# The first projection stage in another order: gates last, the 1/rms row ahead of them, evictions of q, k and v that wait one by one

## The chip, the cores and the metric

The kernel runs on one core of a Trainium2 chip. The metric is the device time of one execution in microseconds. Engines are named as in the profile: PE is TensorE, DVE is VectorE, ACT is ScalarE, POOL is GpSimd, SP is SyncE, whose queue issues most DMAs.

## What is computed

One encoder block on x of 1024 positions by 1024 channels, float32. The part around the change is the beginning:

```python
h = rms_norm(x, norm_mix)
proj = h @ w_in                                  # 1024 x 3104
q, k, v, z, b_f, b_b, a_f, a_b, su, sv = split(proj, [512]*4 + [8]*4 + [512]*2)
qkv = silu(short_conv([q, k, v], conv_w))        # 5 taps along the positions
o_a = bidir_gated_deltanet(qkv, z, b_f, b_b, a_f, a_b, ...)   # 8 heads x 64, chunks of 64
o_b = spatial_gating(su, sv, ...)                # 4 groups x 128, chunks of 128
x = x + [o_a, o_b] @ w_out
x = x + square(relu(rms_norm(x, norm_ffn) @ w_ff1)) @ w_ff2
return rms_norm(x, norm_final)
```

The four small columns b and a (32 in all) are the gates. In the DeltaNet each chunk needs a decay matrix from the gates, Gram products of q and k, and a triangular solve.

## The kernel before

Every large product is done as three float32r matmuls (`mm3`: high x high, high x low, low x high), since each operand is split into a rounded high part and a rest. The rms norm is not applied to x: the products run on x times the gain, and the results are scaled by 1/rms when they leave PSUM. For q, k and v, which come with channels on the partitions, that takes a row of 1/rms for 1024 positions on all partitions, `rrow`.

**First stage** (`first`, L214). Eight steps over the contraction (`dt`). Each loads a piece of x transposed (512 KB, split into `xh` and `xl`) and a piece of weights `w0` (416 columns: 128 each of q, k, v of head pair 0, and the 32 gate columns). x is squared on ACT and summed on DVE into `sqs`. The eight PSUM banks are all taken: `qkv[0..5]` (q, k, v, two halves of the positions each) and `gate[0..1]`. In each step PE does the gates' six matmuls and then 18 for q, k, v. Behind the last step: eight matmuls with a column of ones sum the squares over the partitions (L259), POOL takes the power -0.5 (L262), DVE multiplies the identity with it (`dg`, L265), and two matmuls of a full matrix of ones with `dg` make the row (L272), both into the bank `gate[0]`, copied out by L273. The gates are transposed (L269) and scaled (L275).

**Projections** (`project`, L301). The other columns in the order z, pair 1 (q, k, v), pair 2, a, pair 3, b, where a and b are the two halves of the gating unit's columns. A z, a or b item has eight blocks of 24 matmuls, a q, k or v item two. A block uses one bank of a ring of three (`psd`), and its eviction is put into program order when the block behind it is issued (`flush(1)`). q, k and v are evicted by DVE times `rrow` (`evac_qkv`, L379) into a buffer `cx` of which there are two, z and a, b by ACT. Before a q, k or v item the program waits until the convolution two items back has read its buffer (`self.taps`). Weights come through `piece` (L152): SP loads a raw tile (two buffers), ACT writes the high part and the negated copy, and a POOL DMA adds the source onto it (L164); there are nine buffers `w`. With `early=True` POOL subtracts instead (L149).

**Side lanes.** `conv` (four taps of DVE, L472, behind ACT's first, L469), `heads` (transposes, L495), `gates`, `prep` (decay matrices: matmul L561, exponential L562), `stage1` (Gram products L594, then the solve: L611, L619, 30 steps of L625 and L627, transposes L635 and L637, merge L645 and L657) are generators that say what they cost. `run` lays them beside the projections by those costs, and the scheduler of the framework then orders each engine's queue by priorities and by what is ready in its own model of time. The solves of the four pairs follow one another. `outproj` starts when all of them are done. Then comes the MLP.

The lines that wait and evict before:

```python
yield lambda: n < 0 or n in self.taps      # at the start of a q, k, v item; n = p * 3 + j - 2
...
late.append((self.evac_qkv, ps, x, h, p, j))
flush(1)
```

Of the kernel before, what the change touches and what calls it, by code (L numbers as in the profile page):

```python
# [10 lines left out]
F32 = mybir.dt.float32  # L11
# [3 lines left out]
ALU = mybir.AluOpType  # L15
# [4 lines left out]
P = 128  # L20
# [33 lines left out]
class Kern:  # L54
# [159 lines left out]
    def first(self, xp):  # L214

        nc, a, tkx, tkp = self.nc, self.a, self.tkx, self.tkp
        N = 3 * P + 32
        tmp = tkp.tile([P, 1024], F32, tag="V", name="tmp")
# [23 lines left out]
        self.w0 = [self.piece(a["wt"][0, dt]) for dt in range(NT)]  # L242
        gT = tmp[0:32]
        for dt in range(NT):
            for h in range(2):
                th = slice(h * 512, h * 512 + 512)
                self.mm3(gate[h][0:32], w[dt][:, 0, 3 * P:N], w[dt][:, 1, 3 * P:N], self.xh[dt][:, th], self.xl[dt][:, th],
                         dt == 0, dt == NT - 1)
                if dt == NT - 1:
                    nc.vector.tensor_copy(gT[:, th], gate[h][0:32])  # L250
            for i in range(6):
                j, h = divmod(i, 2)
                ws, th = slice(j * P, j * P + P), slice(h * 512, h * 512 + 512)
                self.mm3(qkv[i], w[dt][:, 0, ws], w[dt][:, 1, ws], self.xh[dt][:, th], self.xl[dt][:, th],
                         dt == 0, dt == NT - 1)
                if dt == NT - 1 and i == 1:

                    for b in range(NB):
                        nc.tensor.matmul(gate[0][:, b:b + 1], sqs[:, b * P:(b + 1) * P], ones[:, 0:1], start=True, stop=True)  # L259
                    with self.tc.high_priority(offset=400):  # L260
                        nc.vector.tensor_scalar(ss, gate[0][:, 0:NB], 1.0 / D, EPS, ALU.mult, ALU.add)
                        nc.gpsimd.tensor_tensor(self.rstd, ss, self.mhalf.broadcast_to([P, NB]), ALU.pow)  # L262

                        dg = self.sgup.tile([P, NB, P], F32, tag="uv", name="dg", bufs=3)
                        nc.vector.tensor_tensor(dg, self.ident.unsqueeze(1).broadcast_to([P, NB, P]),  # L265
                                                self.rstd.unsqueeze(2).broadcast_to([P, NB, P]), ALU.mult)
                if dt == NT - 1 and i == 2:
                    for b in range(NB):
                        nc.tensor.transpose(gate[1][:, b * 32:b * 32 + 32], gT[:, b * P:b * P + P], self.ident[0:32, 0:32])  # L269
# [18 lines left out]
    def new_cx(self):  # L288
# [3 lines left out]
        return x  # L292

    def third(self):

        yield "dve 1.4"
        x = self.new_cx()
        for h in range(2):
            self.evac_qkv(self.qkv0[4 + h], x, h, 0, 2)

    def project(self):  # L301

        nc = self.nc
        late, self.taps, self.uv = [], set(), 3
# [4 lines left out]
        def loads(kind, p, j):  # L309

            if kind == "q":
                return [self.a["wqkv"][p * 3 + j][:, i * 4:i * 4 + 4] for i in range(2)]
            return [self.a["wt"]["zab".index(kind), dt] for dt in range(NT)]

        def flush(n):
            while len(late) > n:
                f, *args = late.pop(0)
                f(*args)

        for j in range(2):  # L320
            yield "dve 1.4"
            x = self.new_cx()
            for h in range(2):
                self.evac_qkv(self.qkv0[j * 2 + h], x, h, 0, j)
        self.side("conv", self.third())
# [6 lines left out]
        for it, (kind, p, j) in enumerate(items):  # L332
            nxt = []
            after = loads(*items[it + 1]) if it + 1 < len(items) else []
            if kind == "q":
                n = p * 3 + j - 2
                yield lambda: n < 0 or n in self.taps
                todo = after
                for h in range(2):
                    yield "pe 2.6" + (" act 2.4" if todo else "")  # L340
                    load(4 - h)
                    if h == 0:
                        x = self.new_cx()
                    ps = self.psd()
                    th = slice(h * 512, h * 512 + 512)
                    for dt in range(NT):
                        if dt == NT // 2:
                            yield "pe 2.6 dve .6"
                        wd, ws = w[dt // 4], slice(dt % 4 * P, dt % 4 * P + P)
                        self.mm3(ps, wd[:, 0, ws], wd[:, 1, ws], self.xh[dt][:, th], self.xl[dt][:, th],  # L350
                                 dt == 0, dt == NT - 1)
                    late.append((self.evac_qkv, ps, x, h, p, j))
                    flush(1)
            else:
# [3 lines left out]
                for b in range(NB):  # L358
# [17 lines left out]
        flush(0)  # L376

    def evac_qkv(self, ps, x, h, p, j):
        self.nc.vector.tensor_tensor(x[:, 2 + h * 512:514 + h * 512], ps, self.rrow[:, h * 512:h * 512 + 512],  # L379
                                     ALU.mult)  # L380
        if h == 1:
            self.side("conv", self.conv(p, j, x))

# [160 lines left out]
    def prep(self, p):  # L544
# [669 lines left out]
def layouts(i):  # L1214
# [9 lines left out]
    dtile = lambda m, n: c(m.reshape(n, NT // n, P, -1).transpose(0, 2, 1, 3))  # L1224
    r["w0"] = c(np.concatenate([w[:, 0:P], w[:, 512:512 + P], w[:, 1024:1024 + P], w[:, 2048:2080]], 1).reshape(NT, P, -1))
    r["wqkv"] = c(np.stack([dtile(w[:, j * 512 + p * P:j * 512 + (p + 1) * P], 1)[0]
# [34 lines left out]
```

## Time and profile before

| | us |
|---|---|
| median of 3 runs | 1374.23 |
| lowest, highest | 1369.28, 1379.46 |
| the profiled execution | 1376.48 |
| its span, first to last instruction | 1374.7 |
| PE busy | 1312.6 |
| DVE busy | 722.4 |
| ACT busy | 516.7 |
| POOL busy | 245.1 |

The profile is of one execution. A busy time counts an engine's instructions and says nothing of which of them the end waited for; times in the rows are counted from the start of the span. A bracket at the end of a row of the order of time gives the idle time of the engine ahead of the instruction, and what ended it.

### The profile page before, as it was taken

The numbers are of one execution on the slowest core, as the hardware profiler recorded it, in microseconds if no ns is written. First come the engines' busy times: TensorE is split into PE (matmuls) and PEld (weight loads), VectorE is DVE, ScalarE is ACT, GpSimd is POOL, SyncE is SP. The second block draws the span as 40 slices with busy tenths as digits, with TensorE's granted clock in tenths as the row PEclk, the third lists the DMA queues.
The fourth block names the chain that finished last, engine by engine and source line by source line (L and its number), as shares of the span: only waits on it lengthen the run. The fifth ranks groups of instructions, "written<-read, shape, count | busy, mean of one in ns | idle before, by whom it ended". The sixth has DMA issues, their size and how long they took to land.

```text
span 1374.7 us, 20558 instructions
## 1 busy us (share of the span) xinstructions
PE 1312.6 (95%) x8129; PEld 1082.6 (79%) x8129; DVE 722.4 (53%) x1213; ACT 516.7 (38%) x958; POOL 245.1 (18%) x353
## 2 busy tenths in 40 slices
PE   8799899999868899999999999999999999999997
PEld 5588687778767798877788888888888888888885
DVE  6252696969696566777533433434333343343445
ACT  6445755587446554413421311313113131131224
POOL 3301330333385776000000000000000000000013
PEclk9899999999979999999999999999999999999999
DMA  6618753572555653410012101121011210212103
GB/s 230 150 45 256 189 139 73 136 156 70 169 145 113 156 134 90 137 47 1 9 46 69 54 23 54 46 69 54 12 58 54 69 45 10 69 54 69 39 16 130
DMA packets 132464, 119.80 MB, mean 87 GB/s; under 512 B 76144, under 2 KB 96496, under 8 KB 131824
## 3 DMA queue, kind: packets, MB, share of 16 engines
q1 hardware_dynamic: 125168, 105.38, 25.4%
q0 software_dynamic: 6048, 11.01, 5.0%
q10 hardware_dynamic: 1152, 2.10, 0.4%
q8 instruction: 64, 1.05, 0.3%
q14 instruction: 32, 0.26, 0.1%
HBM read 91.71 MB, written 27.33 MB: 87 GB/s over the span
## 4 chain that ended last, share of the span: by engine, by line
PE 79%; DVE 7%; ACT 4%; DMA 4%; issue 2%; POOL 2%; SPq 1%; POOLq 0%; ACTq 0%; DVEq 0%
PE psd L140 14%; PE psd L141 14%; PE psd L142 13%; PE psg L140 9%; PE psg L141 9%; PE psg L142 9%; PE psg L805 3%; PE psg L796 2%; DMA raw<-in_wqkv 1%; DVE lt L625 1%; DVE lane L627 1%; PE pss L850 1%; DVE ca L472 1%; DMA raw<-in_wt 1%; PE psg L594 1%
## 5 line engine op out<-in xcount | busy, mean ns | idle before, releaser
L140 PE MATMUL psg<-fh,w 128*128 128x512 f32 x512 | 199.2, 389 | 0.6 <-DVE fl L1017 0.6
L142 PE MATMUL psd<-w,ff 128*128 128x512 f32 x512 | 199.3, 389 | 0.0
L141 PE MATMUL psd<-w,ff 128*128 128x512 f32 x512 | 199.2, 389 | 0.0
L141 PE MATMUL psg<-fl,w 128*128 128x512 f32 x512 | 199.1, 389 | 0.0
L142 PE MATMUL psg<-fh,w 128*128 128x512 f32 x512 | 198.0, 389 | 0.0
L140 PE MATMUL psd<-w,ff 128*128 128x512 f32 x512 | 195.3, 389 | 0.0
L1091 DVE SCALAR_TENSOR_TENSOR x<-psd,r,x 128x512 f32<-128x512 f32 x128 | 94.5, 749 | 175.7 <-PE psd L142 175.6
L148 ACT CAST w<-raw 128x512 fp32r<-128x512 f32 (+2 forms) x104 | 77.6, 746 | 247.9 <-PE psd L142 125.6
L149 DVE TENSOR_TENSOR w<-raw,w 128x512 fp32r<-128x512 f32 (+1 forms) x96 | 83.5, 870 | 101.2 <-ACT w L148 100.9
L1074 ACT ACTIVATE relu<-psg 128x512 f32<-128x512 f32 x64 | 38.2, 597 | 245.8 <-PE psg L142 245.8
L1049 POOL TENSOR_SCALAR fs<-fs 128x1 f32<-128x1 f32 x8 | 5.6, 694 | 672.0 <-ACT scr L1046 672.0
L140 PEld LDWEIGHTS psg<-fh,w 128*128 128x128 f32 x512 | 96.2, 188 | 20.8 <-DVE fl L1017 0.8
L140 PEld LDWEIGHTS psd<-w,ff 128*128 128x128 f32 x512 | 96.1, 188 | 20.3 <-DVE x L1091 0.4
L141 PEld LDWEIGHTS psd<-w,ff 128*128 128x128 f32 x512 | 96.2, 188 | 20.0
L141 PEld LDWEIGHTS psg<-fl,w 128*128 128x128 f32 x512 | 96.2, 188 | 19.9
L142 PEld LDWEIGHTS psg<-fh,w 128*128 128x128 f32 x512 | 96.1, 188 | 19.9
L142 PEld LDWEIGHTS psd<-w,ff 128*128 128x128 f32 x512 | 96.1, 188 | 20.0
L1075 DVE TENSOR_TENSOR relu<-relu 128x512 f32<-128x512 f32 x64 | 44.2, 691 | 110.3 <-ACT relu L1074 110.3
L140 PE MATMUL psd<-xh,w 128*128 128x512 f32 (+1 forms) x168 | 67.4, 404 | 9.9 <-ACT xh L209 5.5
L140 PE MATMUL psd<-w,xh 128*128 128x512 f32 x192 | 76.6, 400 | 0.0
L141 PE MATMUL psd<-w,xh 128*128 128x512 f32 x192 | 76.2, 397 | 0.0
L142 PE MATMUL psd<-w,xl 128*128 128x512 f32 x192 | 76.1, 396 | 0.0
(238 smaller groups left out, 2424.6 us busy)
## 6 DMA issues: line engine op xcount, KB each, us to landing
raw<-in_w SPq DMA_DIRECT2D x32, 512.0 KB, 3.5
raw<-in_w SPq DMA_DIRECT2D x64, 256.0 KB, 2.7
raw<-in_wt SPq DMA_DIRECT2D x24, 256.0 KB, 3.0
w<-in_wt POOLq DMA_DIRECT2D x24, 256.0 KB, 5.1
tok_d<-tok SPq DMA_DIRECT2D x24, 256.0 KB, 4.8
raw<-in_wqkv SPq DMA_DIRECT2D x18, 256.0 KB, 4.1
w<-in_wqkv POOLq DMA_DIRECT2D x18, 256.0 KB, 5.8
t_d<-zero SPq DMA_DIRECT2D x8, 512.0 KB, 9.7
```

The source lines that it names most:

```text
L140: mm(ps, lh, rh, start=start, stop=False)
L141: mm(ps, lh, rl, start=False, stop=False)
L142: mm(ps, ll, rh, start=False, stop=stop)
L148: nc.scalar.copy(w[:, 0], raw)
L149: lo.tensor_tensor(w[:, 1], raw, w[:, 0].bitcast(F32), ALU.subtract)
L472: nc.vector.scalar_tensor_tensor(acc, x[:, t:t + S], cw[:, t:t + 1], acc, ALU.mult, ALU.add)
L594: nc.tensor.matmul(ps[c * 64:c * 64 + 64, b * 64:b * 64 + 64], cm[1][hs, ch], cm[w][hs, ch], start=True, stop=True)
L796: nc.tensor.matmul(pu[:, (r * 2 + t) * P:(r * 2 + t + 1) * P], Tr[:, r, t], vke[:, t, 0:2 + r:1 + r], start=True, stop=True)
L805: nc.tensor.matmul(ps[:, (r * 2 + t) * P:(r * 2 + t + 1) * P], l[:, r, t], uw[:, r, t], start=True, stop=True)
L1074: nc.scalar.activation(r, pf, AF.Relu)
L1075: nc.vector.tensor_tensor(r, r, r, ALU.mult)
L1091: nc.vector.scalar_tensor_tensor(x1[b][:, ns], pf, r4[:, b:b + 1], x1[b][:, ns], ALU.mult, ALU.add)
```

## The change

The gates' weights become one piece of their own, `wg` (8 x 32 columns), loaded behind the eight pieces `w0`, which shrink to 384 columns. In the first stage the steps do q, k and v alone. The sums of squares come behind the sixth step. The ones-matmuls for the row stand behind the loop, at a priority 30 instructions further ahead, one into each of the two gate banks. Then come the gates, half by half over all eight steps, their copies and the transposes. In the projections the wait for the convolution two items back (and for the eviction of v of pair 0) is taken when q, k or v is evicted, no longer when its item begins, and two evictions are held back behind these items in place of one; the buffer is taken at the eviction too. The order of the items stays. The first decay of pair 0 is announced with a latency of 18 in place of 4.

```diff
-        N = 3 * P + 32
+        N = 3 * P
...
+        wg = self.piece(a["wg"], NT * 32, True)
...
         for dt in range(NT):
-            for h in range(2):
-                th = slice(h * 512, h * 512 + 512)
-                self.mm3(gate[h][0:32], w[dt][:, 0, 3 * P:N], w[dt][:, 1, 3 * P:N], self.xh[dt][:, th], self.xl[dt][:, th],
-                         dt == 0, dt == NT - 1)
-                if dt == NT - 1:
-                    nc.vector.tensor_copy(gT[:, th], gate[h][0:32])
             for i in range(6):
...
-                if dt == NT - 1 and i == 1:
+            if dt == NT - 3:
...
-                if dt == NT - 1 and i == 2:
-                    (transposes of the gates)
-        with self.tc.high_priority(offset=100):
+        with self.tc.high_priority(offset=30):
             for h in range(2):
-                nc.tensor.matmul(gate[0], ones, dg[:, h * 4:h * 4 + 4].rearrange("p b t -> p (b t)"), start=True, stop=True)
-                nc.vector.tensor_copy(self.rrow[:, h * 512:h * 512 + 512], gate[0])
+                nc.tensor.matmul(gate[h], ones, dg[:, h * 4:h * 4 + 4].rearrange("p b t -> p (b t)"), start=True, stop=True)
+                nc.vector.tensor_copy(self.rrow[:, h * 512:h * 512 + 512], gate[h])
+        for h in range(2):
+            th = slice(h * 512, h * 512 + 512)
+            for dt in range(NT):
+                gs = slice(dt * 32, dt * 32 + 32)
+                self.mm3(gate[h][0:32], wg[:, 0, gs], wg[:, 1, gs], self.xh[dt][:, th], self.xl[dt][:, th],
+                         dt == 0, dt == NT - 1)
+            nc.vector.tensor_copy(gT[:, th], gate[h][0:32])
+        for b in range(NB):
+            nc.tensor.transpose(gate[1][:, b * 32:b * 32 + 32], gT[:, b * P:b * P + P], self.ident[0:32, 0:32])
...
     def third(self):
         yield "dve 1.4"
-        x = self.new_cx()
         for h in range(2):
-            self.evac_qkv(self.qkv0[4 + h], x, h, 0, 2)
+            self.evac_qkv(self.qkv0[4 + h], h, 0, 2)
+        self.three = True
...
         def flush(n):
             while len(late) > n:
                 f, *args = late.pop(0)
+                if f == self.evac_qkv and args[1] == 0:
+                    k = args[2] * 3 + args[3] - 2
+                    yield lambda: k in self.taps and self.three
                 f(*args)
...
-                n = p * 3 + j - 2
-                yield lambda: n < 0 or n in self.taps
...
-                    late.append((self.evac_qkv, ps, x, h, p, j))
-                    flush(1)
+                    late.append((self.evac_qkv, ps, h, p, j))
+                    yield from flush(2)
...
-                    flush(1)
+                    yield from flush(1)
...
+    def evac_qkv(self, ps, h, p, j):
+        if h == 0:
+            self.cx = self.new_cx()
...
-        yield "lat 4"
+        yield "lat 4" if p else "lat 18"
```

## Rows read from the trace of the kernel before

**Rows 1.** The page, part 4: the chain that ended last, by engine.

```profile
PE 79%; DVE 7%; ACT 4%; DMA 4%; issue 2%; POOL 2%; SPq 1%; POOLq 0%; ACTq 0%; DVEq 0%
```

**Rows 2.** Stretches: length, then busy of PE, PEld, DVE, ACT, POOL, clock, DMA, GB/s.

```profile
53.60:67.65 14.05, 6.59 (x30) 3.86 (x29) 6.02 (x14) 5.43 (x10) 3.44 (x3) 0.64 0.53 113
67.65:71.26 3.61, 3.61 (x11) 2.78 (x9) 3.54 (x9) 2.04 (x2) 0.00 (x0) 0.51 0.00 0
71.26:115.00 43.74, 43.74 (x202) 36.35 (x201) 17.36 (x24) 19.86 (x30) 3.13 (x9) 1.00 0.28 93
115.00:365.00 250.00, 239.44 (x2058) 194.46 (x2058) 186.35 (x333) 155.47 (x242) 68.89 (x92) 0.99 0.56 143
365.00:480.00 115.00, 90.70 (x1125) 81.10 (x1118) 80.94 (x175) 62.59 (x180) 78.73 (x129) 0.90 0.58 145
480.00:600.00 120.00, 119.56 (x1058) 103.25 (x1057) 83.75 (x185) 55.95 (x153) 52.36 (x70) 0.99 0.42 114
```

**Rows 3.** PE in order of time behind the first stage: start, us, instruction.

```profile
53.60 1.84 PE L259 MATMUL psd<-ones,sqs 128*128 128x1 f32 x16
55.37 0.68 PE L269 MATMUL psg<-cst,tmp 32*128 32x32 f32 x8
61.10 2.07 PE L272 MATMUL psd<-dg,ones 128*128 128x512 f32 x2 [5.05 <-DVE dg L265]
65.58 2.07 PE L272 MATMUL psd<-dg,ones 128*128 128x512 f32 x2 [2.41 <-DVE rrow L273]
```

**Rows 4.** VectorE in order of time, from the first stage to the last solve.

```profile
26.96 3.44 DVE L238 TENSOR_TENSOR sqs<-sqs,sq 128x1024 f32<-128x1024 f32 x2
...
60.97 0.42 DVE L275 TENSOR_TENSOR sml<-psg,rstd 128x256 f32<-128x256 f32 x1
...
65.64 0.68 DVE L379 TENSOR_TENSOR cx<-psd,rrow 128x512 f32<-128x512 f32 x1
...
70.55 1.28 DVE L472 SCALAR_TENSOR_TENSOR ca<-cx,smallc,ca 128x1024 f32<-128x1024 f32 x1
...
82.13 0.28 DVE L419 SCALAR_TENSOR_TENSOR tmp<-tmp,sml 128x128 f32<-128x128 f32 x1
...
147.51 2.06 DVE L611 STREAM_TRANSPOSE lane<-n 128x1024 f32<-128x1024 f32 x1 [0.61 <-ACT n L609]
...
419.89 2.02 DVE L637 STREAM_TRANSPOSE VT<-lane 128x1024 f32<-128x1024 f32 x1
```

**Rows 5.** PE in order of time: the gates in step 3, starts of the groups.

```profile
20.71 0.39 PE L140 MATMUL psd<-xh,w 128*32 128x512 f32 x1
...
22.10 0.39 PE L140 MATMUL psd<-xh,w 128*128 128x512 f32 x1
...
26.18 0.39 PE L140 MATMUL psd<-xh,w 128*32 128x512 f32 x1
```

**Rows 6.** ScalarE in order of time: the fourth weight piece.

```profile
22.46 0.53 ACT L148 CAST w<-raw 128x416 fp32r<-128x416 f32 x1
```

**Rows 7.** GpSimd in order of time: subtracts, first and last accumulation for z, a wait.

```profile
23.07 4.93 POOL L149 TENSOR_TENSOR w<-raw,w 128x416 fp32r<-128x416 f32 x2 [7.33 <-ACT w L148]
...
36.94 1.08 POOL L164 DMA_DIRECT2D w<-in_wt  x1 [1.25 <-ACT w L163]
...
54.84 0.86 POOL L164 DMA_DIRECT2D w<-in_wt  x1 [1.29 <-issue]
...
142.66 0.87 POOL L164 DMA_DIRECT2D w<-in_wqkv  x1 [7.40 <-ACT w L163]
```

**Rows 8.** DMA issues from 30 to 66 us: KB each, us to landing.

```profile
w<-in_wt POOLq DMA_DIRECT2D x8, 256.0 KB, 4.7
```

**Rows 9.** Stretches: the first stage's end; the last columns are DMA share and GB/s.

```profile
40.00:60.00 20.00, 16.05 (x85) 12.57 (x83) 1.70 (x4) 9.04 (x15) 8.60 (x9) 0.94 0.97 206
```

**Rows 10.** PE's waits from 100 to 480 us: total us, times, longest.

```profile
PE psd L140 <- DVE cx L379: 2.2, 1, 2.2
```

**Rows 11.** PE in order of time: pair 0's first decay and first Gram products.

```profile
111.13 0.40 PE L561 MATMUL psg<-dr,dl 96*128 96x512 f32 x1
...
125.38 1.15 PE L594 MATMUL psg<-ca,cm 64*64 64x64 f32 x32
```

More of the change, by code (lines that the diff above doesn't have):

```diff
@@ L240, in first @@
                 self.late_consts()
-        self.w0 = [self.piece(a["wt"][0, dt]) for dt in range(NT)]
+        wg = self.piece(a["wg"], NT * 32, True)
+        self.w0 = [self.piece(i) for i in self.pieces("z", 1, 0)]
         gT = tmp[0:32]
         for dt in range(NT):
-            for h in range(2):
-                th = slice(h * 512, h * 512 + 512)
-                self.mm3(gate[h][0:32], w[dt][:, 0, 3 * P:N], w[dt][:, 1, 3 * P:N], self.xh[dt][:, th], self.xl[dt][:, th],
-                         dt == 0, dt == NT - 1)
-                if dt == NT - 1:
-                    nc.vector.tensor_copy(gT[:, th], gate[h][0:32])
             for i in range(6):
@@ L255, in first @@
                          dt == 0, dt == NT - 1)
-                if dt == NT - 1 and i == 1:
[L258 to L266, printed above, removed]
@@ L267, in first @@
-                if dt == NT - 1 and i == 2:
-                    for b in range(NB):
-                        nc.tensor.transpose(gate[1][:, b * 32:b * 32 + 32], gT[:, b * P:b * P + P], self.ident[0:32, 0:32])
-        with self.tc.high_priority(offset=100):
-            for h in range(2):
-                nc.tensor.matmul(gate[0], ones, dg[:, h * 4:h * 4 + 4].rearrange("p b t -> p (b t)"), start=True, stop=True)
-                nc.vector.tensor_copy(self.rrow[:, h * 512:h * 512 + 512], gate[0])
+            if dt == NT - 3:
+                for b in range(NB):
+                    nc.tensor.matmul(gate[0][:, b:b + 1], sqs[:, b * P:(b + 1) * P], ones[:, 0:1], start=True, stop=True)
+                with self.tc.high_priority(offset=400):
+                    nc.vector.tensor_scalar(ss, gate[0][:, 0:NB], 1.0 / D, EPS, ALU.mult, ALU.add)
+                    nc.gpsimd.tensor_tensor(self.rstd, ss, self.mhalf.broadcast_to([P, NB]), ALU.pow)
+                    dg = self.sgup.tile([P, NB, P], F32, tag="uv", name="dg", bufs=3)
+                    nc.vector.tensor_tensor(dg, self.ident.unsqueeze(1).broadcast_to([P, NB, P]),
+                                            self.rstd.unsqueeze(2).broadcast_to([P, NB, P]), ALU.mult)
@@ L274, in first @@
+        for b in range(NB):
+            nc.tensor.transpose(gate[1][:, b * 32:b * 32 + 32], gT[:, b * P:b * P + P], self.ident[0:32, 0:32])
         gt = sml[:, 256:512].rearrange("p (b c) -> p b c", b=NB)
@@ L292, in new_cx, with pieces @@
         return x
+    def pieces(self, kind, p, j):
+        if kind == "q":
+            return [self.a["wqkv"][p * 3 + j][:, i * 4:i * 4 + 4] for i in range(2)]
+        return [self.a["wt"]["zab".index(kind), dt] for dt in range(NT)]
     def third(self):
         yield "dve 1.4"
-        x = self.new_cx()
         for h in range(2):
-            self.evac_qkv(self.qkv0[4 + h], x, h, 0, 2)
+            self.evac_qkv(self.qkv0[4 + h], h, 0, 2)
+        self.three = True
     def project(self):
         nc = self.nc
-        late, self.taps, self.uv = [], set(), 3
+        late, self.taps, self.uv, self.three = [], set(), 3, False
         items = []
@@ L307, in project @@
             items += [("q", int(c), j) for j in range(3)] if c.isdigit() else [(c, 0, 0)]
[L309 to L313, printed above, removed]
         def flush(n):
@@ L333, in project @@
             nxt = []
-            after = loads(*items[it + 1]) if it + 1 < len(items) else []
+            after = self.pieces(*items[it + 1]) if it + 1 < len(items) else []
             if kind == "q":
-                n = p * 3 + j - 2
-                yield lambda: n < 0 or n in self.taps
                 todo = after
@@ L1224, in layouts @@
     dtile = lambda m, n: c(m.reshape(n, NT // n, P, -1).transpose(0, 2, 1, 3))
-    r["w0"] = c(np.concatenate([w[:, 0:P], w[:, 512:512 + P], w[:, 1024:1024 + P], w[:, 2048:2080]], 1).reshape(NT, P, -1))
+    r["w0"] = c(np.concatenate([w[:, 0:P], w[:, 512:512 + P], w[:, 1024:1024 + P]], 1).reshape(NT, P, -1))
+    r["wg"] = c(w[:, 2048:2080].reshape(NT, P, 32).transpose(1, 0, 2).reshape(P, -1))
     r["wqkv"] = c(np.stack([dtile(w[:, j * 512 + p * P:j * 512 + (p + 1) * P], 1)[0]
```

12 lines of the change are left out of this document (4 added, 8 removed).

## The prediction

> **What bounds the kernel now.** I read four views in this order. The chain that ended last is PE for 79% of the span [rows 1], so a microsecond in which PE has nothing to do counts, unless PE would have waited later anyway. The table of stretches [rows 2] says where PE has nothing to do. From 480 us to the end it is practically full: 119.56 of 120 us up to 600 us, and the stretch behind is the MLP. Three places are left: 53.60 to 67.65 us with 6.59 us busy of 14.05, 115 to 365 us with 239.44 of 250, and 365 to 480 us with 90.70 of 115. From 71.26 to 115 us PE does the z projection without a gap.
>
> The third view is PE's order of time in the first of these places [rows 3]. The first stage's products end at 53.60 us. Then come the eight small matmuls that sum the squares (1.84 us) and the transposes of the gates (0.68 us), and PE sits for 5.05 us until VectorE has made `dg`, the diagonal matrix of 1/rms. The first ones-matmul of L272 runs, PE waits 2.41 us for the copy that empties its only bank, the second one runs, and z begins. Each of the two takes 2.07 us, at a granted clock of 0.64 over the stretch. For the next 3.61 us, now on z, the clock is 0.51, the 1.2 GHz level; from 71.26 us the rows show 1.00 again [rows 2]. So the hole has a price behind its end too.
>
> The fourth view is VectorE [rows 4]. Its triangular solves follow one another from 147.51 us (L611 of pair 0) to 421.9 us (the last L637, 419.89 + 2.02), and the output projection starts only when they are through. VectorE is busy 186.35 us of the 250 us from 115 to 365 us. That is why PE's idle time there and up to 480 us isn't free to be taken: if the solves don't end earlier, time won on PE is waited away before 480 us.
>
> **The change, part by part.**
>
> *The gates leave the loop.* Forty-eight matmuls with 32 output columns move from inside the eight steps to behind them. Six of them take 22.10 - 20.71 = 1.39 us and a whole step of 24 takes 26.18 - 20.71 = 5.47 us [rows 5], so a step becomes 4.1 us and the moved block is 48 x 0.232 = 11.1 us. Nothing of it is removed. PE only reaches each step's weights earlier. For the fourth step that matters: it would begin at 26.18 less 18 gate matmuls, about 22.0 us, but its weights' high half is written only at 22.46 + 0.53 = 23.0 us [rows 6]. The low half follows from GpSimd (two subtracts in 4.93 us from 23.07 us, the first of them near 25.5 us) and enters only one product in three [rows 7]. I take 1.0 us of waiting; the bounds are 0 and 3.6 us, should the low half bind.
>
> *The 1/rms row goes ahead.* The squares are summed by 26.96 + 3.44 = 30.4 us [rows 4]. The sums come after the sixth step (near 35 us) instead of after the eighth, so the chain through GpSimd's power and `dg`, for which PE waited 5.05 us, runs beside steps seven and eight, 8.2 us of matmuls. The two ones-matmuls have a bank each, so the wait of 2.41 us for the copy has no cause any more. At the full clock they take half of 2.07 us each. The row is then finished some 10 us ahead of the gates, and the four evictions of q and k (0.68 us each) are done beside the gate block [rows 4].
>
> *The sum.* New end of the first stage: 53.60 + 1.0 (waiting for weights) + 1.84 (sums) + 2.07 (both ones-matmuls) + 0.68 (transposes) = 59.2 us, taking the gates' copy for covered by z's first matmuls (0.7 us if it isn't). Before, z begins for good at 67.65 us and loses half of 3.61 us to the clock, as if it began at 69.45 us. Gain: 10.3 us, with bounds of 7 and 11.5 us.
>
> *Its loads.* The eight weight pieces shrink from 208 to 192 KB and a ninth of 128 KB appears, so bytes and converted columns stay equal (8 x 416 = 8 x 384 + 256). The ninth goes through SP's queue, ScalarE and GpSimd ahead of z's eight pieces, and takes a ninth weight buffer, so that piece i of z now waits for step i, not i - 1; steps end before the pieces come. Pieces of z follow each other every (54.84 - 36.94) / 7 = 2.56 us, and the last is issued for accumulation at 54.84 us and lands 0.86 + 4.7 us later, at 60.4 us [rows 7, 8]. One more piece ahead moves that to at most 63.0 us. z needs it after seven eighths of its first block, 59.2 + 4.8 = 64.0 us. I take nothing, with 1.0 us to spare; a further pitch of delay would cost 1.6 us.
>
> The DMA engines were 0.97 busy from 40 to 60 us, while SP's loads and GpSimd's accumulations of the same pieces ran together [rows 9]. The Trainium skill ("DMA: Bandwidth & Descriptors", section "Issuing engines are not separate DMA queues") says that transfers from different issuing engines end up on the same 16 engines and interleave. That agrees with the share, and it speaks against the change: PE arrives earlier, the weights don't. This is the third rival below.
>
> *Evictions of q, k, v wait singly.* Before, a projection item waits at its start until the convolution two items back has freed its buffer, and one eviction is held back. Now matmuls go ahead, two evictions are held back, and only the eviction waits. PE hardly waited for these: one wait of 2.2 us for an eviction [rows 10]. The other side is that an eviction now comes one block of 5.5 us later in program order, with three banks in the ring, and that the memsets of the new buffer move with it into GpSimd's queue, behind weight transfers that wait (one of them 7.40 us for ScalarE [rows 7]). The trace before cannot price this. Bounds: a gain of the 10.56 us that PE is idle from 115 to 365 us [rows 2], and a loss of 2.2 us for each of 18 blocks, 39.6 us. I take 0, because the nearest row is a single wait.
>
> *Longer latency written for the first decay.* It only shifts where pair 0's first decay matmul is put. That ran at 111.13 us, inside the last block of z, and pair 0's Gram products at 125.38 us [rows 11]. If it keeps its place against z, it costs nothing.
>
> *Carry to the end.* The gates are ready for VectorE at about 60.5 us, against 60.97 us. Before, from there to the gates' last step at 82.13 us, VectorE also did two row copies, four evictions and some eight taps of 1.2 us [rows 4], about 14 of 21 us. Those come earlier now, so the gates' end comes earlier by more than the 10 us, and the decay can follow z. Then the first solve, and all solves behind it, move with z. So nothing is late next before 480 us, and the sum stands: 1376.48 us (the profiled execution; its span is 1374.7) - 10.3 = 1366.2. The median of the three runs is 1374.23, 2.25 us below the profiled one, so the forecast is **1364 us**.
>
> **Rivals.**
>
> 1. *The solves keep their place.* The hole closes, but the decay of pair 0 is still paced by the gates, which come no earlier at 60.5 us, and by weight loads that ScalarE waits for. Then Gram and solve start at 125 and 147 us as before and PE waits longer between 115 and 480 us. For: 34.9 us of idle PE are there already in these two stretches. Against: the 14 us of other work on VectorE that moves ahead of the gates. Time: 1374 less up to 3 us, 1372.5.
>
> 2. *The eviction edit helps too.* Matmuls run ahead and convolutions and solves get out of each other's way; up to the whole 10.56 us of idle PE from 115 to 365 us go, if the solves shorten as well: down to 1353.5, taken at 1356. For: VectorE has 63.65 us free in that stretch. Against: its convolutions come later, not earlier.
>
> 3. *z waits for its weights.* The accumulations get no faster under more load. Two pitches late, 5.1 us, less the 1.0 us to spare, gives 4.1 us back: 1368.
>
> 4. *Banks run out* (slower). With two evictions held back and three banks, a block can begin only when the eviction of the third block back is done, and that is queued behind taps and solve steps. At 2.2 us a block, 18 blocks lose 39.6 us: 1364 + 39.6 = 1403.6. It makes the kernel slower from five blocks on (11 us against 10.3), and by over 1% from eleven.
>
> 5. *The row isn't ahead.* If the ones-matmuls end up behind the gates in PE's order, evictions start when z should; the row's copies and first evictions, about 2.6 us, and a second drop of the clock, 1.8 us, come back: 1368.4.
>
> **How the numbers follow.** Chances: forecast 0.45, its own range 1360 to 1368; rival 1, 0.20; rival 2, 0.18; rivals 3 and 5 together, 0.11; rival 4, 0.06. The range runs from the lower end of rival 2 to the upper side of rival 1 with the spread of the runs: 1353 to 1376, which leaves out rival 4 and little else. One per cent, 13.7 us, is about what a measurement of this kernel tells from no change. Faster by more than that (below 1360.5): rival 2 and a fifth of the forecast's chance, 0.27. Slower by more than that: most of rival 4, 0.05. Within: 0.68.
>
> **What the profile after would show.** Right: no wait of PE for `dg` or for a row copy; ones-matmuls of about 1 us each inside or right behind the last step; gate matmuls from near 47 to 58.5 us; z from 59 to 60 us with the clock at 1.00; the first solve near 137 us and the last transpose near 411 us. Rival 1: z early but the last transpose still near 421 us. Rival 2: less than 10 us of idle PE from z's end to the last q, k, v block. Rival 3: PE waiting for DMA or the accumulated weights in z's first block. Rival 4: many waits of PE for L379's evictions. Wrong altogether would be an order in which the solves of two pairs stand further apart than before, for which no row of before gives a price.

## The result and the profile after

| | before | after |
|---|---|---|
| median, us | 1374.2 (1369.28 to 1379.46) | 1352.47 (1352.0 to 1353.48) |
| ratio, 95% interval | | 0.984 (0.9808 to 0.9872) |
| the profiled execution | 1376.48 | 1353.48 |
| its span | 1374.7 | 1351.7 |
| PE busy, PE idle within the span | 1312.6, 62.1 | 1306.1, 45.6 |

The change makes the kernel 1.6% faster, about 22 us where 10 were forecast, and the median lies just under the low end of the range. The count of PE's time splits it: PE is idle 16.5 us less and busy 6.5 us less, although the matmuls are the same. Of the 6.5 us, 4.6 show in the rows as matmuls that ran at the lower clock before: 2.1 us in the two groups of ones-matmuls (2.07 us each, 1.02 after), 2.5 us in the first nine of z (below). The rest was not traced.

In the profile after, most line numbers stand one higher than in the rows of before. The same stretches as in [rows 2], with the same columns:

```profile
53.60:67.65 14.05, 13.82 (x66) 9.64 (x65) 12.04 (x12) 7.50 (x9) 2.00 (x6) 1.00 0.53 111
115.00:365.00 250.00, 237.49 (x2112) 194.31 (x2112) 187.32 (x343) 160.35 (x254) 80.21 (x111) 0.97 0.57 147
365.00:480.00 115.00, 104.24 (x1252) 95.85 (x1248) 84.22 (x198) 64.97 (x195) 83.41 (x128) 0.92 0.55 134
```

The first line is the hole, gone: 13.82 us busy for 6.59, at clock 1.00 for 0.64. The stretch from 115 us has not become fuller. The one from 365 us has, from 90.70 to 104.24 us; the stage that fills it begins at 361.57 us there and at 383.59 us before (below). PE in order of time in the first stage, against [rows 3]:

```profile
22.30 0.50 PE L140 MATMUL psd<-xh,w 128*128 128x512 f32 x1 [1.73 <-ACT w L148]
...
34.77 1.84 PE L254 MATMUL psd<-ones,sqs 128*128 128x1 f32 x16
...
44.32 1.02 PE L264 MATMUL psd<-dg,ones 128*128 128x512 f32 x2
...
46.50 0.39 PE L140 MATMUL psd<-xh,w 128*32 128x512 f32 x1
...
52.05 0.39 PE L140 MATMUL psd<-w,xh 128*128 128x512 f32 x1
...
58.03 0.40 PE L142 MATMUL psd<-w,xl 128*128 128x512 f32 x1
...
65.24 0.68 PE L274 MATMUL psg<-cst,tmp 32*128 32x32 f32 x8 [0.23 <-DVE tmp L272]
```

The fourth step waits 1.73 us for its weights. The ones-matmuls (L264) run at 1.02 us without a wait in front. The gates stand from 46.50 us, with two matmuls of z between their halves, and z runs on from 58.03 us. VectorE over the same time, and its first and last step of the solves, against [rows 4]:

```profile
42.43 1.23 DVE L260 TENSOR_TENSOR dg<-cst,rstd 128x1024 f32<-128x1024 f32 x1 [5.60 <-POOL rstd L257]
...
55.53 1.29 DVE L473 SCALAR_TENSOR_TENSOR ca<-cx,smallc,ca 128x1024 f32<-128x1024 f32 x1 [6.22 <-ACT ca L470]
...
64.51 0.67 DVE L272 COPY tmp<-psg 32x512 f32<-32x512 f32 x1
...
70.06 0.42 DVE L276 TENSOR_TENSOR sml<-psg,rstd 128x256 f32<-128x256 f32 x1
...
80.10 0.29 DVE L420 SCALAR_TENSOR_TENSOR tmp<-tmp,sml 128x128 f32<-128x128 f32 x1
...
138.59 2.03 DVE L612 STREAM_TRANSPOSE lane<-n 128x1024 f32<-128x1024 f32 x1 [6.30 <-ACT n L610]
...
425.34 2.05 DVE L638 STREAM_TRANSPOSE VT<-lane 128x1024 f32<-128x1024 f32 x1
```

The last line is the important one. The first solve begins 8.9 us earlier than before, but the last transpose ends at 427.4 us, 5.5 us **later** than the 421.9 us of before, and the kernel is still 23 us shorter. So the end did not wait for the last solve to come earlier.

Where the time is won is found by following PE to the end of the projections. Behind it the head groups open: each is the DeltaNet's remaining work on one block of positions of one pair (L796 before, L797 after, is its first matmul; its operand `Tr` is a solve's result, read back from memory). Before:

```profile
371.17 0.39 PE L142 MATMUL psd<-w,xl 128*128 128x512 f32 x1
...
376.30 0.58 PE L140 MATMUL psg<-vs,sgw 128*128 128x256 f32 x1 [2.69 <-ACT vs L709]
382.36 0.58 PE L141 MATMUL psg<-vs,sgw 128*128 128x256 f32 x1 [5.48 <-POOL vs L710]
...
383.59 1.84 PE L796 MATMUL psg<-vke,Tr 128*128 128x128 f32 x8
```

And after:

```profile
354.22 0.40 PE L142 MATMUL psd<-w,xl 128*128 128x512 f32 x1
...
361.57 0.77 PE L797 MATMUL psg<-vke,Tr 128*128 128x128 f32 x2 [3.81 <-DMA Tr<-t_d]
```

From the first group matmul to the end of the span are 991.1 us before (1374.7 - 383.59) and 990.1 us after. All but 1 us is won by then. The 23.0 us are therefore four pieces, each the difference of two PE times:

- Start of z: 11.6 us. Before, nine z matmuls at the lower clock take from 66.67 to 71.26 us, where nine at 0.23 us would take 2.07, as if z had begun at 69.19 us. After, it begins at 58.03 us with two matmuls (0.46 us) done already: 57.57 us.
- From there to the last projection matmul: 302.0 before, 296.65 after, 5.3 us.
- From it to the first group matmul: 12.42 before, 7.35 after, 5.1 us. Before, PE stood behind a late matmul of the gating unit that waited 2.69 us for ScalarE and 5.48 us for GpSimd.
- From there to the end: 1.0 us.

Half is the hole that the change closes. The other half lies far behind the first stage, and the experiments ask where it is from.

### The profile page after: what moved, and what is told of

Its sections match the earlier page's. It is cut to its first block, busy times and chain, and to the rows that moved or that the text cites. A ratio compares the mean times of both kernels' runs of the same rounds, so it can differ in the third digit from the quotient of the medians.

```text
span 1351.7 us, 20583 instructions
## 1 busy us (share of the span) xinstructions
PE 1306.1 (97%) x8129; PEld 1081.1 (80%) x8129; DVE 715.6 (53%) x1213; ACT 517.4 (38%) x959; POOL 247.3 (18%) x354
## 4 chain that ended last, share of the span: by engine, by line
PE 72%; DVE 10%; DMA 8%; ACT 3%; POOL 3%; issue 3%; SPq 1%; POOLq 0%; ACTq 0%; DVEq 0%
PE psd L140 13%; PE psd L141 12%; PE psd L142 12%; PE psg L140 9%; PE psg L142 9%; PE psg L141 9%; PE psg L806 2%; DMA raw<-in_wt 2%; DVE lt L626 2%; DMA raw<-in_wqkv 1%; DVE lane L628 1%; DMA t_d<-zero 1%; PE psg L797 1%; DMA raw<-in_w 1%; PE pss L851 1%
## 5 line engine op out<-in xcount | busy, mean ns | idle before, releaser
L148 ACT CAST w<-raw 128x512 fp32r<-128x512 f32 (+3 forms) x105 | 77.7, 740 | 241.2 <-PE psd L142 125.4
L140 PE MATMUL psd<-xh,w 128*128 128x512 f32 (+1 forms) x168 | 66.7, 399 | 7.2 <-ACT xh L209 5.4
## 6 DMA issues: line engine op xcount, KB each, us to landing
t_d<-zero SPq DMA_DIRECT2D x8, 512.0 KB, 11.4
```

The source lines that it names most:

```text
L140: mm(ps, lh, rh, start=start, stop=False)
L148: nc.scalar.copy(w[:, 0], raw)
```

## The experiments

The change has three parts: F, the first stage; E, the evictions that wait singly; L, the latency of 18 (the one line `yield "lat 4" if p else "lat 18"`). For every build the table gives the ratio to before with its 95% interval, and from its profile the start of z (the first of seven z matmuls in a row), the time from there to the last projection matmul, from that to the first group matmul, from that to the end, and the start of the last transpose of the solves (L637, or the line it moved to). All builds compute the same function. The ratio is one of medians; the stages are of one execution each, which lay from 3.6 us below its build's median (E, held) to 9.2 us above it (transposes first), so differences of a few us between stages of two builds are not clear of that.

| build | ratio | z | to last projection | to group | to end | last solve |
|---|---|---|---|---|---|---|
| before | 1 | 66.7 | 304.5 | 12.4 | 991.1 | 419.9 |
| F+E+L, the change | 0.984 (0.9808 to 0.9872) | 58.0 | 296.2 | 7.4 | 990.1 | 425.3 |
| F | 1.0002 (0.9983 to 1.0021) | 58.7 | 315.2 | 8.1 | 993.4 | 418.8 |
| E | 0.9968 (0.9947 to 0.9989) | 66.3 | 310.7 | 4.9 | 985.9 | 427.8 |
| L | 0.9951 (0.9926 to 0.9977) | 67.4 | 296.2 | 5.6 | 999.4 | 417.0 |
| F+E | 0.991 (0.9881 to 0.9939) | 60.5 | 298.5 | 10.0 | 996.7 | 424.1 |
| F+L | 0.9857 (0.9827 to 0.9887) | 62.0 | 296.4 | 4.9 | 996.4 | 409.6 |
| E+L | 0.9999 (0.9983 to 1.0016) | 67.8 | 304.3 | 9.2 | 993.6 | 443.6 |
| F+E, transposes first | 0.9948 (0.9924 to 0.9972) | 60.1 | 313.7 | 8.6 | 993.0 | 429.4 |
| change, latency 30 | 1.0024 (1.0007 to 1.0041) | 59.2 | 306.8 | 4.9 | 1009.0 | 463.9 |
| before, held | 0.9934 (0.9912 to 0.9956) | 68.1 | 303.7 | 5.9 | 992.7 | 435.3 |
| F, held | 0.9933 (0.9906 to 0.996) | 60.8 | 299.4 | 12.9 | 992.6 | 434.6 |
| transposes first, held | 0.997 (0.9953 to 0.9988) | 59.1 | 309.2 | 7.0 | 998.5 | 436.7 |
| F+L, held | 0.9846 (0.9827 to 0.9864) | 58.5 | 292.3 | 4.9 | 997.4 | 407.6 |
| E, held | 1.0011 (0.9994 to 1.0028) | 67.5 | 307.8 | 4.8 | 994.0 | 430.8 |
| before, split | 0.997 (0.9954 to 0.9985) | 68.7 | 303.5 | 12.1 | 989.6 | 420.9 |
| change, latency 17 | 0.9902 (0.9871 to 0.9932) | 58.5 | 305.3 | 7.7 | 992.4 | 435.5 |
| change, latency 21 | 0.9947 (0.9928 to 0.9965) | 60.8 | 306.8 | 6.8 | 996.6 | 455.3 |

### The parts alone and in pairs

First the question was whether the gain is the sum of the parts, all the first stage's, or the latency's. F alone:

> The first stage alone: gates last and the 1/rms row ahead of them, with the evictions and the latency of 4 as before. Parts that add up (my theory): the hole behind the first stage is worth some 10 us and no more, so 1363 us, z from 58 us, the last projection near 361 us. Rival, all of it comes from the first stage and what it sets off later: 1352 us, the last projection near 354 us. Rival, the order that the latency gives decides: 1363 us too, and then the run without the latency tells.

It gives nothing, 1.0002 (median 1376.02 us), which none of the three expectations allows, although its hole closes as in the change: z at 58.7 us. The table says where the 8 us went: 10.7 us more between the start of z and the last projection matmul. PE's waits in that build from 115 to 390 us (in total, times, longest), and its stretch:

```profile
PE psg L646 <- DVE VT L638: 3.8, 1, 3.8
PE psg L797 <- POOL vke L770: 3.7, 1, 3.7
PE psd L140 <- DVE cx L380: 2.6, 1, 2.6
```

```profile
115.00:365.00 250.00, 237.15 (x2041) 192.42 (x2040) 182.39 (x331) 153.62 (x239) 70.09 (x90) 0.95 0.54 140
```

The waits are others than before's. The longest names a solve: a pair's merge (L646) stands in PE's in-order queue ahead of projections and waits for the solve's last transpose. The clock is 0.95 where before had 0.99, and 0.04 of 250 us is 10 us of full speed (an estimate from the two rows), so most of the 10.7 us may be clock. A wait can cost twice, once as a wait and once in the clock. PE in order of time in the change shows how:

```profile
195.92 0.39 PE L142 MATMUL psd<-w,xl 128*128 128x512 f32 x1
198.33 0.79 PE L141 MATMUL psd<-w,xh 128*128 128x512 f32 x1 [2.02 <-DMA w<-in_wt]
198.91 0.63 PE L142 MATMUL psd<-w,xl 128*128 128x512 f32 x1
...
201.85 0.39 PE L140 MATMUL psd<-w,xh 128*128 128x512 f32 x1
```

Behind a wait of 2.02 us eight matmuls take 3.52 us; at 0.23 us each they would take 1.84. This wait costs 3.7 us. Not every wait of this length does (last section).

The other parts and pairs:

> The first stage as before, only the evictions changed (single waits, two held back). Parts that add up: 1363 us, with the hole from 56 to 66 us still there and the last projection near 364 us instead of 371. All from the first stage: 1374 us, the same as before.

> The whole change with the first decay's latency of 4 as before. Parts that add up, and all from the first stage: 1352 us, as the changed kernel, since the latency only shifts one matmul's place in the order. The latency's order decides: 1360 us or more.

> The first stage and the latency of 18, the evictions as before. Parts that add up: 1363 us. All from the first stage: 1352 us. The latency's order decides: 1352 us, with 1363 us for the first stage alone.

> The kernel before with nothing but the first decay's latency of 18 in place of 4. Theory A: the latency lets the transposes of pair 0's q and k, which until now stood behind the first decay in the order of the banks, run during z, at about 95 us instead of 111; this is worth some 13 us by itself, so 1361 us. Theory B: it is worth something only where the first stage has closed its hole, since with the hole PE waits elsewhere: 1372 to 1375 us. Theory C, luck of the order: any time between 1360 and 1385 us.

> The changed kernel with the first stage of before: what the first stage is worth when the two other parts are there. Theory A: the hole of 10 us comes back and nothing else, 1363 us. Theory B, the first stage carries all of it: 1372 us or more. Theory C: any time from 1355 to 1380 us.

The medians are 1371.80 us for E, 1365.66 for F+E, 1357.47 for F+L, 1369.54 for L and 1377.53 for E+L. E lies nearer to its 1374 than to its 1363 us, "the latency's order decides" alone has F+E right (1360 or more), F+L falls between its forecasts, L alone fits theory C only, and E+L fits B and C.

The parts don't add up. In ratios, F is worth +0.0002 on before, -0.0058 on E, -0.0094 on L and -0.0159 on E+L; L is worth -0.0049 on before, -0.0145 on F, +0.0031 on E and -0.007 on F+E. Each of these differences is uncertain by 0.003 to 0.004, so the small ones are no more than zero, and the large ones are clear. No part has a worth of its own that holds in the presence of the others.

### A mechanism for the latency: transposes ahead of the decay

Theory A: with latency 4 the first decay matmul takes a PSUM bank and PE's place ahead of pair 0's first transposes, and these wait with it. Theory B, that the latency is worth something only where the first stage is new, fails already: L alone gives -0.0049 (0.9926 to 0.9977), 1369.54 us against its 1372 to 1375; theory C is that every edit draws another order for the in-order queues, good or bad. PE in order of time, F alone (latency 4):

```profile
106.95 0.40 PE L562 MATMUL psg<-dr,dl 96*128 96x512 f32 x1
107.19 0.60 PE L496 MATMUL psg<-cst,ca 128*128 128x128 f32 x4
```

and the change (latency 18):

```profile
87.41 0.60 PE L496 MATMUL psg<-cst,ca 128*128 128x128 f32 x4
...
106.07 0.40 PE L562 MATMUL psg<-dr,dl 96*128 96x512 f32 x1
```

The transposes come 20 us earlier with 18. One build is F+E with the transposes put first (the first diff, against latency 4), another goes further with the latency:

```diff
+        if p == 0:
+            yield lambda: 0 in self.turned
         yield "lat 4"
```

```diff
-        yield "lat 4" if p else "lat 18"
+        yield "lat 4" if p else "lat 30"
```

> The whole change with a latency of 4, and instead an explicit wait in the program: the first decay is put into order only behind the transposes of pair 0's q. Theory A, the place of these transposes ahead of the decay is what the latency of 18 buys: they run near 87 and 93 us as in the changed kernel, and the time is 1352 to 1357 us, against 1365.66 with the latency of 4 alone. Theory C, luck of the order: about 1366 us or any other time.

> The changed kernel with the first decay's latency at 30. The transposes of q and of k then stand ahead of the decay, and the decay comes some 5 us later. Theory A: the transposes are early enough already, 1352 to 1358 us. Theory C, luck of the order: about as far from 1352 as the latency of 4 is, 1362 us or more.

Transposes at 89.2 us and a first solve at 134.0 us, both about as early as the change has them or earlier, give 0.9948 (1367.94 us, where theory A has 1352 to 1357), no better than F+E without them (0.991). In its profile, an execution 9.2 us above the median, the last projection matmul comes 15 us later than in F+E's. So theory A falls: what the latency did to the transposes is no gain by itself. Latency 30 costs all that was won (1380.16 us). Its last transpose begins at 463.9 us and it takes 1009.0 us from the group to the end, both the largest of the table. That the solves bind there is not shown: PE's waits behind the group name a solve's result (`Tr`) for 2.1 us only, and the clock is 0.82 from 365 to 480 us, against 0.92 in the change.

### A mechanism for the order: pair 2's merge held back

Theory D: side work that PE does ahead of the last projection matmul is paid in full, and behind it hidden by the head groups. Theory S is the prediction's, that the solves set the end. In these builds the merge of pair 2 (the `py` matmuls of L645 or L646) waits for the last projection matmul (`self.projected`, set behind the last `flush`):

```diff
+        yield lambda: p < 2 or self.projected
...
+                if p == 2:
+                    st.enter_context(self.tc.issue_after(self.projected.ins))
```

> The kernel before, with pair 2's merge (the matmuls behind its solve) held on PE until the last projection matmul is issued. Theory D: the head groups open when the projections are over, and from there to the end it always takes some 991 us, so side work that PE does ahead of the last projection is paid in full and side work behind it is hidden: the last projection at 366 us instead of 371, and the time 5 us lower, 1370 to 1371 us. Theory S (my prediction's): the solves set the end; the merge comes later, pair 3's solve with it, and the time is 1378 us or more. Theory C, luck of the order: any other time.

> The first stage alone, with pair 2's merge held in the same way. In the first stage alone all three merges stood ahead of the last projection, and PE waited 3.8 us in front of the third. Theory D: the group start moves from 382 us to 371 us or less, and the time from 1376 to 1366 us. Theory S: 1376 us or more. Theory C: any other time.

> The run with the explicit order of pair 0's transposes and the decay, with pair 2's merge held. Theory D: half of that merge stood ahead of the last projection at 376 us, so the last projection comes 4 us or more earlier and the time is 1363 us, against 1367.94. Theory S: 1368 us or more. Theory C: any other time.

One more run went for the 5.48 us that PE waits before for GpSimd, with a subtraction of the gating unit moved to VectorE:

```diff
-        (nc.vector if (k, h) == (1, 3) else nc.gpsimd).tensor_tensor(vl, v, vh.bitcast(F32), ALU.subtract)
+        (nc.vector if k == 1 and h >= 2 else nc.gpsimd).tensor_tensor(vl, v, vh.bitcast(F32), ALU.subtract)
```

> The kernel before, with the gating unit's last but one subtraction on VectorE instead of GpSimd. PE waited 5.48 us for it between the last projection and the first head group, since GpSimd did the groups' openings ahead of it. Theory D: the groups start 4 to 5 us earlier, and the time is 1370 to 1371 us. Theory S: the time doesn't move, 1375 us, since the solves are what the end waits for. Theory C: any other time.

It moved a subtraction other than the one waited for. The wait stayed (5.4 us), so the run tells nothing of it, though its 1374.54 us is theory S's number.

Theory S falls: before with the hold is 0.66% faster with its last transpose 15 us **later**. Theory D looked good on before and on F (-0.0066 and -0.0069) and not on the third (+0.0022). On before the time was right and the way was not: the last projection matmul stayed at 371.8 us (forecast: 366), and the gain lies behind it, 5.9 us to the group for 12.4. Two more orders, and two builds that leave this mechanism alone and move only the announced latency, were to settle it.

> First stage and latency together, and pair 2's merge held behind the last projection matmul. Theory D (side work ahead of the last projection matmul is paid, behind it the head-group stage hides it): the same gain as the hold gave twice, 8 to 9 us, so 1357.5 - 8.5 = 1349, under the whole change; last projection matmul near 350 us, group stage 5 us behind, 990 us to the end. Theory C (each build draws another order, worth up to 10 us either way): anything from 1348 to 1368.

> The eviction edit alone with pair 2's merge held behind the last projection matmul. Theory D: 1371.8 - 8.5 = 1363. Theory C: anything from 1362 to 1382.

> The whole change with latency 17 in place of 18. One decay matmul of PE trades places with one projection matmul and later places differ here and there (a seventh of what other edits move); the heads stay ahead of the decay. All theories: within 3 us of the whole change, 1350 to 1356. If it is further off, even such a difference of order has a price and theory C gains.

> The whole change with latency 21. Pair 0's first transposes stand one block earlier and the first decay matmul two places earlier, and the later order of all engines differs widely. Theory A/D (what counts is that the transposes go ahead of the waiting decay, which holds here): 1349 to 1356. Theory C: anything from 1348 to 1376, most likely slower than the whole change, as that is the best of the orders seen.

The hold gives -0.0011 on F+L and +0.0043 on E: five orders, from -0.0069 to +0.0043. Theory D falls as a rule. F+L held has the last projection matmul (350.9 us) and the group (4.9 us behind) where theory D put them, but from there it takes 997.4 us, not 990, and is as fast as the change, not faster. Latency 17 (1363.73 us) and 21 (1371.51 us) lie outside every theory but C. Latency 17 is the sharpest case. Decays (L562) and transposes (L496) of PE in order of time, in the change:

```profile
106.07 0.40 PE L562 MATMUL psg<-dr,dl 96*128 96x512 f32 x1
106.30 0.60 PE L496 MATMUL psg<-cst,cm 128*128 128x128 f32 x4
...
123.25 0.66 PE L496 MATMUL psg<-cst,cm 128*128 128x128 f32 x4 [1.23 <-ACT n L563]
```

and with latency 17:

```profile
106.29 0.62 PE L562 MATMUL psg<-dr,dl 96*128 96x512 f32 x2
106.75 0.60 PE L496 MATMUL psg<-cst,cm 128*128 128x128 f32 x4
...
133.85 0.60 PE L496 MATMUL psg<-cst,cm 128*128 128x128 f32 x4
```

With 17 two decay matmuls stand ahead of the first transposes of `cm` instead of one, the third group of four comes 10.6 us later (133.85 us for 123.25), and the queues of all engines differ in places from there on. The first solve comes earlier with 17 (136.8 us against 138.6), the last projection matmul 9.6 us later. PE's waits for weights in the change from 115 to 372 us:

```profile
PE psd L141 <- DMA w<-in_wt: 3.2, 2, 2.0
...
PE psd L142 <- DMA w<-in_wqkv: 0.5, 1, 0.5
```

with latency 17:

```profile
PE psd L141 <- DMA w<-in_wt: 6.0, 2, 4.8
PE psd L142 <- DMA w<-in_wqkv: 3.8, 1, 3.8
```

The waits for the same weights are 6.1 us longer. The next pair of runs shows that they need not go with the order.

Is that the order or the day? The last two builds ran side by side. Latency 15 gives every engine the same order as 17.

```diff
-        yield "lat 4" if p else "lat 18"
+        yield "lat 4" if p else "lat 15"
```

> The whole change once more, on the same chip and beside the same runs of before as latency 15. If orders have prices: ratio 0.984 as the first time, 8 us faster than latency 15. If the 8.5 us between the change and latency 17 came from the chip or the day: both at the same ratio, near 0.987.

> The whole change with latency 15: its engines' order is the same as with 17, which differs from the whole change in a few places. If orders have prices: ratio 0.990 as with 17. If the difference was chance of chip and day: the same ratio as the whole change.

The change again: 1358.31 us, 0.9857 (0.9833 to 0.988). Latency 15: 1363.06 us, 0.9909 (0.9889 to 0.9929). So the difference stays, at 4.8 us where 8 were expected. PE's waits for weights from 115 to 372 us in the change again:

```profile
PE psd L141 <- DMA w<-in_wt: 5.5, 2, 2.9
...
PE psd L142 <- DMA w<-in_wqkv: 0.7, 1, 0.7
```

with latency 15:

```profile
PE psd L141 <- DMA w<-in_wt: 3.7, 2, 3.2
...
PE psd L142 <- DMA w<-in_wqkv: 2.1, 1, 2.1
```

Here the better order waits 6.2 us for weights and the worse one 5.8. These waits change by 2.5 us between two executions of one order and by 4.0 us between two of the other, so they are no measure of the order. The two profiled executions are 1358.79 and 1359.33 us, almost the same; the difference is one of medians.

Both days together, all eight runs of the change lie between 1352.0 and 1358.8 us, and all ten of the other order between 1359.3 and 1369.8 us. A difference of order that no theory here would price is worth 0.5 to 0.6%, 5 to 9 us. Latency 17 or 15 on F+E (0.9902, 0.9909) is worth nothing against latency 4 (0.991); 18 happens to draw a better order.

### What they say together

The 18 builds of the table are 18 orders of the same work. The eleven with the new first stage average 0.9925 (0.984 to 1.0024), the seven without it 0.9976 (0.9934 to 1.0011). The difference is 7 us; with spreads of 8.4 and 3.9 us within the two groups its standard error is about 3 us (8.4 squared over 11 plus 3.9 squared over 7, the root of it). They weren't drawn by chance, so this is a guide, but the hole's 10 to 11 us are within two of these errors. In each build with F, z starts 4 to 11 us earlier than in those without. What happens between there and the last projection matmul adds anything from 292 to 315 us, and that hides or doubles the gain.

## Why the prediction was wrong

**The first stage: right in its mechanism, a little small.** The forecast had 10.3 us with bounds of 7 and 11.5; measured are 11.6. Weights of the fourth step 1.73 us (1.0, bounds 0 and 3.6), sums at 34.77 us (near 35), ones-matmuls 1.02 us each (half of 2.07), gate matmuls over 11.5 us, two of z among them (11.1), z from 58.03 us (59.2, with 0.68 us of transposes counted ahead of it that came inside it, at 65.24 us). Some 1.7 us came from the start of the stage, which the sum doesn't hold. Before:

```profile
7.46 0.63 PE L140 MATMUL psg<-xh,w 128*32 128x512 f32 x1 [0.89 <-ACT xh L209]
```

and the matmuls follow each other at 0.43 us until 13.2 us, then at 0.23; after, there is no such wait, and the slower pace ends at 10.7 us.

**The third rival's weights: right not to take.** z starts without a wait for its accumulated pieces.

**The gates: wrong.** They were to be ready for VectorE at 60.5 us; their scaling (L276) runs at 70.06 us against 60.97 before, since both copies of the gates stand in VectorE's queue behind convolution taps of 1.3 us. The gates' end was to come earlier by more than 10 us; their last step (L420) begins at 80.10 us against 82.13, 2.0 us. The first decay runs at 106.07 us, 5.1 us earlier than before, and so does not follow z. No price of this is seen by itself.

**The evictions: 0 was as good as any.** E is worth -0.0032 alone, -0.0092 on F, +0.0048 on L and -0.0017 on F+L. The bounds, -10.56 and +39.6 us, hold these (at most 12.6 us of gain), but for a little at the lower end. Rival 4, banks that run out, has no row in the waits of the change; the nearest is one wait of 4.1 us for an eviction (L380) with latency 30.

**The latency: "if it keeps its place against z, it costs nothing".** The decay matmul came 48.0 us behind the start of z (106.07 - 58.03) where it had come 44.5 us behind it. The step failed: the order of all queues changed with it, and the line moved the kernel by -0.0145 to +0.0031, depending on what else was in.

**"Carry to the end": the step that failed.** It said that the first solve, and all solves behind it, move with z, so that the first stage's 10.3 us are the whole sum and everything behind it adds nothing; and that time won on PE is waited away before 480 us if the solves don't move. The first solve came nearly as forecast (138.6 us, near 137), in part by luck, as the gates and the decay ahead of it had moved by 2.0 and 5.1 us only. The solves behind it did not move with it. The four begin 8.9 and 16.4 us earlier, 7.3 us later and 6.0 us earlier; the third, before and after:

```profile
300.05 2.03 DVE L611 STREAM_TRANSPOSE lane<-n 128x1024 f32<-128x1024 f32 x1 [3.48 <-PE psg L658]
307.30 2.01 DVE L612 STREAM_TRANSPOSE lane<-n 128x1024 f32<-128x1024 f32 x1
```

The last transpose was to end near 411 us and ended at 427.4, and by the text's own sign that was rival 1, no gain. It was the largest gain of all builds, and in the profile 11.4 of its 23.0 us came from behind the start of z. In 19 of 20 profiles from the first group matmul to the end are 986 to 999 us, while the last transpose begins anywhere from 408 to 455 us (the twentieth, latency 30, has 1009 us and 463.9). Over the 20 the span goes with the **last projection matmul** on PE's in-order queue (correlation 0.83; 1 would be in step, 0 not at all), much less with the last transpose (0.45) or the start of z (0.44). That is what the runs show in the failed step's place; that this matmul alone sets the end they don't, as the piece behind the group still differs by 13 us. [Rows 2] showed 10.56 us of idle PE ahead of 365 us and 24.3 behind; the prediction took both for waits on the solves, without looking at what each waits for. PE's longest waits before, from 115 to 390 us, and the only one that names a solve:

```profile
PE psg L141 <- POOL vs L710: 5.8, 2, 5.5
PE psg L805 <- ACT uw L798: 3.8, 1, 3.8
PE psg L140 <- ACT vs L709: 2.7, 1, 2.7
...
PE psg L645 <- DVE bl L618: 0.7, 1, 0.7
```

Further on, the last solve does stand on the chain that ended last before, but PE waits only 1.59 us where that chain comes back to it:

```profile
437.42 1.13 PE L796 MATMUL psg<-vke,Tr 128*128 128x128 f32 x8 [1.59 <-DMA Tr<-t_d]
```

So the forecast had a size for the hole and no price for the order. That the eleven builds with F average 0.9925, which is the 1364 us of the forecast, is in part luck: F alone, which is what the sum priced, gave nothing. The prediction named "an order in which the solves of two pairs stand further apart than before" as what would make it wrong altogether, and left it out for want of a row. That is the order that came: from the first solve to the last transpose are 286.8 us after and 272.4 before. But it came with a gain. The builds give the missing row: with the first stage new, a spread of 8 us around the mean.

**What stays open.** Which of the many places in which two orders differ costs how much. Early transposes, the held merge and the announced latency were tried as causes, and none keeps its sign. Waits for weights were longer in one execution of the worse order and shorter in another. The transition's wait for GpSimd was not tried on the right subtraction.

## What to carry to other kernels

When an edit goes through a planner and a scheduler, price the stage that it closes from rows, and then ask which instruction ends the overlapped stretch: follow PE to it, and not the busiest helper. Give the reordering of everything behind it a spread of its own, measured by a build or two that change nothing but an announced cost, before a gain or a loss of under 1% is put down to a mechanism. A part that gives nothing alone (F, 1.0002) and much in company may have worked both times.

## What the runs showed of the hardware

Two executions of one program can differ by several us at one mean granted clock (0.982 to 0.986): the change ran in 1352.0 to 1353.5 us five times and in 1358.2 to 1358.8 us three times, and nothing between. In the profiles of one of each, waits for weight DMAs on PE from 115 to 372 us are 3.7 and 6.2 us in total.

A wait's price beyond itself is seen at 198.33 us (above): 2.02 us of waiting, then 1.7 us lost at a granted clock of 0.51, the lower of the two levels. The other execution of the same program waits longer at the same matmul, and the clock stays at 1.00:

```profile
201.39 0.50 PE L141 MATMUL psd<-w,xh 128*128 128x512 f32 x1 [2.57 <-DMA w<-in_wt]
201.72 0.39 PE L142 MATMUL psd<-w,xl 128*128 128x512 f32 x1
```

In the kernel before, matmuls follow each other at 0.23 us behind a wait of 2.20 us (274.08 us) and at 0.43 us behind one of 2.17 us (279.25 us). So the length of such a wait alone does not tell what it costs in the clock.
